# Instance normalisation over 64 tiles: six loads and six stores in turn, and a two-pass variance by pairs of tiles

## The chip, the cores and the metric

The kernel runs on one core of one Trainium2 chip. The metric is the device time in microseconds (us) of that core; lower is better. All runs compared here are with a granted clock of 1.0. A core has engines that run side by side: TensorE (PE in the profile), VectorE (DVE), ScalarE (ACT), GpSimd (POOL) and SyncE (SP). Here SP issues all DMAs, on one queue. Sixteen DMA engines do the moving. VectorE takes its instructions in the order in which the build put them; SP issues its DMAs in program order.

## The reference

```python
x = np.random.randn(8, 64, 32, 64, 64).astype(np.float32)      # 268 MB
mean = np.mean(x, axis=(2, 3, 4), keepdims=True)
var = np.var(x, axis=(2, 3, 4), keepdims=True)
out = (x - mean) / np.sqrt(var + 1e-5)
```

There are 512 instances (batch times channel) of 131,072 elements. Both kernels put 8 instances in a tile of 128 partitions by 8192 float32, which is 4 MiB, so there are 64 tiles. Every tile is loaded once and stored once.

## The kernel before

One tile is a group. Its sum (VectorE) and its sum of squares (ScalarE) are taken side by side, straight from the tile. A matmul with a block matrix adds the 16 partitions of each instance. A few small steps give scale and bias, and the normalising is shared by three engines. There are four tile buffers, and SP issues loads and stores alternately, with a store two tiles behind its load. The code is cut; `...` marks what is left out.

```python
c1 = F // 8; c2 = F // 4
norm_splits = [(nc.vector, 0, c1), (nc.scalar, c1, c2), (nc.gpsimd, c2, F)]
...
def issue_compute(g, x_tiles):
    for k in range(KPG):                                   # KPG is 1
        nc.vector.reduce_sum(out=psums[:, k, 0:1], in_=x_tiles[:, k, :], axis=...X)
        nc.scalar.activation(out=sq_scratch, in_=x_tiles[:, k, :], func=...Square,
                             accum_out=psums[:, k, 1:2])
    nc.tensor.matmul(out=tot, lhsT=ones_t, rhs=psums, start=True, stop=True)
    # ... mean, E[x^2] + eps - mean^2, square root, reciprocal, bias
    for eng, lo, hi in norm_splits: ...                    # x * scale + bias, in place
...
for g in range(n_groups):
    x_tiles = issue_load(g)
    issue_compute(g, x_tiles)
    pending[g] = x_tiles
    if g >= LAG:                                           # LAG is 2
        issue_store(g - LAG, pending.pop(g - LAG))
```

## Time and profile before

| | before |
|---|---|
| time, median | 1251.46 us (1250.81 to 1252.0, 3 runs) |
| span of the profiled run | 1249.7 us |
| DMA queue q1, share of 16 engines | 99.7% |
| moved | 536.88 MB, 430 GB/s |
| busiest compute engine | VectorE, 53% |

These are lines of the page of before: busy time, the queue line (packets, MB, share of the 16 engines' span), the chain of waits by engine, and three groups of instructions. A group's columns are: line, engine, operation, names, shapes and count; then busy us and the mean ns of one; then idle us before it and what ended that.

```profile
PE 35.7 (3%) x128; PEld 32.1 (3%) x128; DVE 659.2 (53%) x449; ACT 550.6 (44%) x258; POOL 380.3 (30%) x70
...
q1 hardware_dynamic: 18432, 536.88, 99.7%
...
DMA 74%; issue 16%; POOL 7%; DVE 1%; POOLq 1%; PE 0%; ACT 0%
...
L92 DVE TENSOR_REDUCE psums<-x_tiles 128x1 f32<-128x8192 f32 x64 | 555.9, 8686 | 492.9 <-DMA x_tiles<-in_x_dram 492.9
L100 ACT ACTIVATE sq_scratch<-x_tiles 128x8192 bf16<-128x8192 f32 x64 | 449.9, 7029 | 461.3 <-DMA x_tiles<-in_x_dram 461.3
L169 POOL TENSOR_SCALAR x_tiles<-x_tiles,scale,bias 128x6144 f32<-128x6144 f32 x64 | 379.4, 5929 | 855.4 <-DVE bias L149 634.4
```

The DMA engines are the bound: the queue is busy for 99.7% of the span, while VectorE and ScalarE sit waiting for loads.

The next lines are the chain of waits of before in order of time (start us, length us, what). They cover one period of four loads and four stores.

```profile
1023.82 31.48 DMA out_dram<-x_tiles
1055.30 0.02 issue
1055.32 26.52 DMA x_tiles<-in_x_dram
1081.84 13.26 issue
1095.10 0.04 POOLq L169
1095.15 0.12 issue
1095.27 5.95 POOL x_tiles L169
1101.21 0.02 issue
1101.23 31.49 DMA out_dram<-x_tiles
```

From 1023.82 to 1101.23 is 77.41 us for eight transfers of 4 MiB, so one transfer takes 9.68 us, and twelve would take 116.1 us. That pace is what a change would have to beat, or keep.

### The profile page before, as it was taken

The page shows a single profiled execution, that of the slowest core. Times are in us where ns is not written, and L with a number is a line of the kernel's source. Part 1 is how long each engine was busy: PE and PEld are TensorE (multiplying, and loading weights), DVE is VectorE, ACT ScalarE, POOL GpSimd, SP SyncE. Part 2 cuts the span into 40 slices and gives each one's busy share as a digit, 9 for nine tenths or more (in the row PEclk, how much of TensorE's full clock was granted, in tenths as well). Part 3 has the DMA queues.
Part 4 walks back from the last instruction along what each step waited for, and adds up shares of the span by engine and source line. Part 5 has one row for each costly group of instructions (what it writes and reads, how often), then busy time and mean ns, then how long its engine had stood idle before and what let it go on. Part 6 is the DMA issues. An engine that isn't in the chain of part 4 may idle for free.

```text
span 1249.7 us, 1827 instructions
## 1 busy us (share of the span) xinstructions
PE 35.7 (3%) x128; PEld 32.1 (3%) x128; DVE 659.2 (53%) x449; ACT 550.6 (44%) x258; POOL 380.3 (30%) x70
## 2 busy tenths in 40 slices
PE   0000000000000000000000000000000000000000
PEld 0000000000000000000000000000000000000000
DVE  5736455464554645546546455464554645646543
ACT  5535445354453544535435344354453544534432
POOL 2332332313323233232331322313323233132231
DMA  9999999999999999999999999999999999999998
GB/s 403 417 434 434 427 433 430 432 435 430 429 432 434 432 435 429 434 433 434 434 431 433 431 434 434 435 430 432 434 433 436 429 433 434 433 434 435 429 433 357
DMA packets 18444, 536.99 MB, mean 430 GB/s; under 512 B 2048, under 2 KB 2048, under 8 KB 2048
## 3 DMA queue, kind: packets, MB, share of 16 engines
q1 hardware_dynamic: 18432, 536.88, 99.7%
q14 instruction: 11, 0.09, 0.0%
q8 instruction: 1, 0.02, 0.0%
HBM read 268.44 MB, written 268.44 MB: 430 GB/s over the span
## 4 chain that ended last, share of the span: by engine, by line
DMA 74%; issue 16%; POOL 7%; DVE 1%; POOLq 1%; PE 0%; ACT 0%
DMA out_dram<-x_tiles 39%; DMA x_tiles<-in_x_dram 35%; POOL x_tiles L169 7%; DVE psums L92 1%; POOLq L221 0%; DVE x_tiles L169 0%; POOLq L169 0%; PE tot L108 0%; ACT std L141 0%; DVE scale L147 0%; DVE msq L128 0%; DVE me L117 0%; DVE bias L149 0%; DVE var_eps L131 0%
## 5 line engine op out<-in xcount | busy, mean ns | idle before, releaser
L92 DVE TENSOR_REDUCE psums<-x_tiles 128x1 f32<-128x8192 f32 x64 | 555.9, 8686 | 492.9 <-DMA x_tiles<-in_x_dram 492.9
L100 ACT ACTIVATE sq_scratch<-x_tiles 128x8192 bf16<-128x8192 f32 x64 | 449.9, 7029 | 461.3 <-DMA x_tiles<-in_x_dram 461.3
L169 POOL TENSOR_SCALAR x_tiles<-x_tiles,scale,bias 128x6144 f32<-128x6144 f32 x64 | 379.4, 5929 | 855.4 <-DVE bias L149 634.4
L161 ACT ACTIVATE x_tiles<-x_tiles,bias,scale 128x1024 f32<-128x1024 f32 x64 | 79.4, 1241 | 40.5 <-DVE bias L149 40.5
L141 ACT ACTIVATE std<-var_eps 128x1 f32<-128x1 f32 x64 | 13.0, 203 | 178.7 <-DVE var_eps L131 178.7
L108 PE MATMUL tot<-psums,ones_t 128*128 128x2 f32 x128 | 35.7, 348 | 1193.5 <-DVE psums L92 1193.5
L108 PEld LDWEIGHTS tot<-psums,ones_t 128*128 128x128 f32 x128 | 32.1, 311 | 1197.1 <-issue 1197.1
L169 DVE TENSOR_SCALAR x_tiles<-x_tiles,scale,bias 128x1024 f32<-128x1024 f32 x64 | 52.1, 813 | 2.5
L117 DVE TENSOR_SCALAR me<-tot 128x2 f32<-128x2 f32 x64 | 10.2, 160 | 47.5 <-PE tot L108 47.5
L147 DVE RECIPROCAL scale<-std 128x1 f32<-128x1 f32 x64 | 10.5, 164 | 21.8 <-ACT std L141 21.8
L100 ACT ACTIVATION_READ_ACCUMULATOR sq_scratch<-x_tiles 128x1 f32 x64 | 11.9, 187 | 0.0
L128 DVE TENSOR_TENSOR msq<-me 128x1 f32<-128x1 f32 x64 | 10.2, 159 | 2.2
L131 DVE SCALAR_TENSOR_TENSOR var_eps<-me,msq 128x1 f32<-128x1 f32 x64 | 10.2, 159 | 2.2
L149 DVE SCALAR_TENSOR_TENSOR bias<-me,scale 128x1 f32<-128x1 f32 x64 | 10.2, 159 | 2.2
L100 ACT ACT_TABLE_LOAD x1 | 1.3, 1283 | 0.8 <-PEq L207 0.8
L141 ACT ACT_TABLE_LOAD x1 | 1.3, 1283 | 0.0
L51 DVE MEMSET ones_t<- 128x128 f32 x1 | 0.2, 165 | 0.9 <-PEq L207 0.9
L53 POOL TENSOR_SCALAR_AFFINE_SELECT ones_t<-ones_t 128x128 f32<-128x128 f32 x1 | 0.3, 343 | 0.6 <-DVE ones_t L51 0.6
L62 POOL TENSOR_SCALAR_AFFINE_SELECT ones_t<-ones_t 128x128 f32<-128x128 f32 x1 | 0.3, 338 | 0.1
L207 POOL MEMSET const-float32-0.0<- 128x1 f32 x1 | 0.1, 98 | 0.3 <-issue 0.3
L207 POOL MEMSET const-bfloat16-1.0<- 128x1 bf16 x1 | 0.1, 101 | 0.0
L207 POOL MEMSET const-uint8-127<- 128x1 uint8 x1 | 0.1, 101 | 0.0
(1 smaller groups left out, 0.1 us busy)
## 6 DMA issues: line engine op xcount, KB each, us to landing
x_tiles<-in_x_dram SPq DMA_DIRECT2D x64, 4096.0 KB, 29.0
out_dram<-x_tiles SPq DMA_DIRECT2D x64, 4096.0 KB, 31.5
```

What stands on the lines that cost most here:

```text
L92: nc.vector.reduce_sum(out=psums[:, k, 0:1], in_=x_tiles[:, k, :], axis=mybir.AxisListType.X,)
L100: nc.scalar.activation(out=sq_scratch, in_=x_tiles[:, k, :], func=mybir.ActivationFunctionType.Square, accum_out=psums[:, k, 1:2],)
L108: nc.tensor.matmul(out=tot, lhsT=ones_t, rhs=psums, start=True, stop=True,)
L117: nc.vector.tensor_scalar(out=me2, in0=tot, scalar1=inv_F, scalar2=None, op0=mybir.AluOpType.mult,)
L128: nc.vector.tensor_mul(out=msq, in0=mean, in1=mean)
L131: nc.vector.scalar_tensor_tensor(out=var_eps, in0=e2, scalar=eps_f, in1=msq, op0=mybir.AluOpType.add, op1=mybir.AluOpType.subtract,)
L141: nc.scalar.activation(out=std, in_=var_eps, func=mybir.ActivationFunctionType.Sqrt,)
L147: nc.vector.reciprocal(out=scale, in_=std)
L149: nc.vector.scalar_tensor_tensor(out=bias, in0=mean, scalar=-1.0, in1=scale, op0=mybir.AluOpType.mult, op1=mybir.AluOpType.mult,)
L161: nc.scalar.activation(out=x_tiles[:, k, lo:hi], in_=x_tiles[:, k, lo:hi], func=mybir.ActivationFunctionType.Identity, scale=scale[:, k : ...
L169: eng.tensor_scalar(out=x_tiles[:, k, lo:hi], in0=x_tiles[:, k, lo:hi], scalar1=scale[:, k : k + 1], scalar2=bias[:, k : k + 1], op0=mybir ...
L207: nc = _bacc.Bacc("TRN2", target_bir_lowering=False, num_devices=1)
```

## The change

The intent is to keep the DMA in one direction for longer (six tiles in, six tiles out, six buffers), to use the safer two-pass variance, and to split the work by engine: VectorE sums, ScalarE squares, GpSimd normalises. Statistics are taken for two tiles at a time. The diff is cut to its core.

```diff
-    data_pool = ctx.enter_context(tc.tile_pool(name="data", bufs=4))
+    SLOTS = 6
+    BATCH = 2
+    data_pool = ctx.enter_context(tc.tile_pool(name="data", bufs=SLOTS))
 # ...
+    def compute(batch):
+        for k, t in enumerate(batch):
+            nc.vector.reduce_sum(out=sums[:, k : k + 1], in_=t, axis=...X)
+        nc.tensor.matmul(out=mean_ps, lhsT=avg, rhs=sums, start=True, stop=True)
+        nc.vector.tensor_scalar(out=neg_mean, in0=mean_ps, scalar1=-1.0, ..., op0=Alu.mult)
+        for k, t in enumerate(batch):
+            nc.scalar.activation(out=unused, in_=t, func=Act.Square,
+                                 bias=neg_mean[:, k : k + 1],
+                                 accum_out=squares[:, k : k + 1])
+        nc.tensor.matmul(out=var_ps, lhsT=avg, rhs=squares, start=True, stop=True)
+        nc.scalar.activation(out=std, in_=var_ps, func=Act.Sqrt, bias=eps_t)
+        nc.vector.reciprocal(out=scale, in_=std)
+        for k, t in enumerate(batch):
+            nc.gpsimd.tensor_scalar(out=t, in0=t, scalar1=neg_mean[:, k : k + 1],
+                                    scalar2=scale[:, k : k + 1], op0=Alu.add, op1=Alu.mult)
 # ...
+    loaded, stored = 0, 0
+    while stored < n_tiles:
+        load_and_compute(range(loaded, min(stored + SLOTS, n_tiles)))
+        loaded = min(stored + SLOTS, n_tiles)
+        turn = n_tiles % SLOTS or SLOTS if stored == 0 else SLOTS
+        for g in range(stored, stored + turn):
+            store(g, tiles.pop(g))
+        stored += turn
```

On SP this gives 6 loads, 4 stores, 4 loads, 6 stores, and then nine full turns of 6 loads and 6 stores. A pair is two tiles whose statistics are taken together, "sum3" is the sum of the third tile of a turn, and "recip12" is the reciprocal of the first pair.

More of the change, by code (lines that the diff above doesn't have):

```diff
@@ L4 @@
 import concourse.tile as tile
-from concourse import bass_utils, mybir
+from concourse import mybir
 from concourse._compat import with_exitstack
@@ L18 @@
     fp32 = mybir.dt.float32
+    Alu = mybir.AluOpType
+    Act = mybir.ActivationFunctionType
     P = 128
@@ L29 @@
     F = n_elem // SPLIT
-    G = 8
-    KPG = G // IPT
-    n_groups = n_inst // G
-    LAG = 2
-    x_packed = x.rearrange("b c d h w -> (b c) (d h w)").rearrange(
+    n_tiles = n_inst // IPT
+    SLOTS = 6
+    BATCH = 2
+    x_t = x.rearrange("b c d h w -> (b c) (d h w)").rearrange(
         "(k i) (s f) -> k (i s) f", i=IPT, s=SPLIT
     )
-    out_packed = out.rearrange("b c d h w -> (b c) (d h w)").rearrange(
+    out_t = out.rearrange("b c d h w -> (b c) (d h w)").rearrange(
         "(k i) (s f) -> k (i s) f", i=IPT, s=SPLIT
@@ L44 @@
     singles = ctx.enter_context(tc.tile_pool(name="singles", bufs=1))
-    data_pool = ctx.enter_context(tc.tile_pool(name="data", bufs=4))
-    scratch_pool = ctx.enter_context(tc.tile_pool(name="scratch", bufs=2))
+    data_pool = ctx.enter_context(tc.tile_pool(name="data", bufs=SLOTS))
     stat_pool = ctx.enter_context(tc.tile_pool(name="stats", bufs=4))
-    psum_pool = ctx.enter_context(tc.tile_pool(name="psum", bufs=4, space=bass.MemoryType.PSUM))
-    ones_t = singles.tile([P, P], fp32)
-    nc.vector.memset(ones_t, 1.0 / SPLIT)
-    blk_pattern = [[-SPLIT, P // SPLIT], [0, SPLIT]]
+    psum_pool = ctx.enter_context(
+        tc.tile_pool(name="psum", bufs=2, space=bass.MemoryType.PSUM)
+    )
+    avg = singles.tile([P, P], fp32, name="avg")
+    nc.vector.memset(avg, 1.0 / n_elem)
     nc.gpsimd.affine_select(
-        out=ones_t,
-        in_=ones_t,
-        pattern=blk_pattern,
-        compare_op=mybir.AluOpType.is_ge,
+        out=avg,
+        in_=avg,
+        pattern=[[-SPLIT, IPT], [0, SPLIT]],
+        compare_op=Alu.is_ge,
         fill=0.0,
@@ L62 @@
     nc.gpsimd.affine_select(
-        out=ones_t,
-        in_=ones_t,
-        pattern=[[SPLIT, P // SPLIT], [0, SPLIT]],
-        compare_op=mybir.AluOpType.is_ge,
+        out=avg,
+        in_=avg,
+        pattern=[[SPLIT, IPT], [0, SPLIT]],
+        compare_op=Alu.is_ge,
         fill=0.0,
@@ L70 @@
     )
-    inv_F = 1.0 / F
-    c1 = F // 8
-    c2 = F // 4
-    norm_splits = [
-        (nc.vector, 0, c1),
-        (nc.scalar, c1, c2),
-        (nc.gpsimd, c2, F),
-    ]
-    def issue_load(g):
-        x_tiles = data_pool.tile([P, KPG, F], fp32, name="x_tiles")
-        src = x_packed[g * KPG : (g + 1) * KPG].rearrange("k p f -> p k f")
-        nc.sync.dma_start(out=x_tiles, in_=src)
-        return x_tiles
-    def issue_compute(g, x_tiles):
-        psums = stat_pool.tile([P, KPG, 2], fp32, name="psums")
-        for k in range(KPG):
+    eps_t = singles.tile([P, 1], fp32, name="eps_t")
@@ L92, in issue_compute, with load, store @@
+    nc.vector.memset(eps_t, eps_f)
+    unused = singles.tile([P, F], mybir.dt.uint8, name="unused")
+    def load(g):
+        t = data_pool.tile([P, F], fp32, name="xt")
+        nc.sync.dma_start(out=t, in_=x_t[g])
+        return t
+    def store(g, t):
+        nc.sync.dma_start(out=out_t[g], in_=t)
+    def compute(batch):
+        n = len(batch)
+        sums = stat_pool.tile([P, n], fp32, name="sums")
+        for k, t in enumerate(batch):
             nc.vector.reduce_sum(
-                out=psums[:, k, 0:1],
@@ L94, in issue_compute @@
-                in_=x_tiles[:, k, :],
-                axis=mybir.AxisListType.X,
-            )
-            sq_scratch = scratch_pool.tile(
-                [P, F], mybir.dt.bfloat16, name="sq_scratch"
-            )
-            nc.scalar.activation(
-                out=sq_scratch,
-                in_=x_tiles[:, k, :],
-                func=mybir.ActivationFunctionType.Square,
-                accum_out=psums[:, k, 1:2],
-            )
-        tot = psum_pool.tile([P, KPG, 2], fp32, name="tot")
@@ L108, in issue_compute @@
-        nc.tensor.matmul(
-            out=tot,
-            lhsT=ones_t,
-            rhs=psums,
-            start=True,
-            stop=True,
-        )
-        me2 = stat_pool.tile([P, KPG, 2], fp32, name="me2")
-        nc.vector.tensor_scalar(
-            out=me2,
-            in0=tot,
-            scalar1=inv_F,
-            scalar2=None,
-            op0=mybir.AluOpType.mult,
-        )
-        mean = me2[:, :, 0]
-        e2 = me2[:, :, 1]
-        msq = stat_pool.tile([P, KPG], fp32, name="msq")
@@ L128, in issue_compute @@
-        nc.vector.tensor_mul(out=msq, in0=mean, in1=mean)
-        var_eps = stat_pool.tile([P, KPG], fp32, name="var_eps")
-        nc.vector.scalar_tensor_tensor(
-            out=var_eps,
-            in0=e2,
-            scalar=eps_f,
-            in1=msq,
-            op0=mybir.AluOpType.add,
-            op1=mybir.AluOpType.subtract,
-        )
-        std = stat_pool.tile([P, KPG], fp32, name="std")
-        nc.scalar.activation(
-            out=std,
-            in_=var_eps,
-            func=mybir.ActivationFunctionType.Sqrt,
-        )
@@ L146, in issue_compute @@
-        scale = stat_pool.tile([P, KPG], fp32, name="scale")
-        nc.vector.reciprocal(out=scale, in_=std)
-        bias = stat_pool.tile([P, KPG], fp32, name="bias")
-        nc.vector.scalar_tensor_tensor(
-            out=bias,
-            in0=mean,
-            scalar=-1.0,
-            in1=scale,
-            op0=mybir.AluOpType.mult,
-            op1=mybir.AluOpType.mult,
-        )
-        for k in range(KPG):
-            for eng, lo, hi in norm_splits:
-                if eng is nc.scalar:
-                    nc.scalar.activation(
-                        out=x_tiles[:, k, lo:hi],
-                        in_=x_tiles[:, k, lo:hi],
-                        func=mybir.ActivationFunctionType.Identity,
-                        scale=scale[:, k : k + 1],
-                        bias=bias[:, k : k + 1],
-                    )
-                else:
-                    eng.tensor_scalar(
-                        out=x_tiles[:, k, lo:hi],
-                        in0=x_tiles[:, k, lo:hi],
-                        scalar1=scale[:, k : k + 1],
-                        scalar2=bias[:, k : k + 1],
-                        op0=mybir.AluOpType.mult,
-                        op1=mybir.AluOpType.add,
-                    )
@@ L178, in issue_store @@
-    def issue_store(g, x_tiles):
-        dst = out_packed[g * KPG : (g + 1) * KPG].rearrange("k p f -> p k f")
-        nc.sync.dma_start(out=dst, in_=x_tiles)
-    pending = {}
-    for g in range(n_groups):
-        x_tiles = issue_load(g)
-        issue_compute(g, x_tiles)
-        pending[g] = x_tiles
-        if g >= LAG:
-            issue_store(g - LAG, pending.pop(g - LAG))
-    for g in range(n_groups - LAG, n_groups):
-        issue_store(g, pending.pop(g))
+                out=sums[:, k : k + 1], in_=t, axis=mybir.AxisListType.X
+            )
@@ new lines, in compute @@
+        mean_ps = psum_pool.tile([P, n], fp32, name="mean_ps")
+        nc.tensor.matmul(out=mean_ps, lhsT=avg, rhs=sums, start=True, stop=True)
+        neg_mean = stat_pool.tile([P, n], fp32, name="neg_mean")
+        nc.vector.tensor_scalar(
+            out=neg_mean, in0=mean_ps, scalar1=-1.0, scalar2=None, op0=Alu.mult
+        )
+        squares = stat_pool.tile([P, n], fp32, name="squares")
+        for k, t in enumerate(batch):
+            nc.scalar.activation(
+                out=unused,
+                in_=t,
+                func=Act.Square,
+                bias=neg_mean[:, k : k + 1],
+                accum_out=squares[:, k : k + 1],
+            )
@@ new lines, in compute @@
+        var_ps = psum_pool.tile([P, n], fp32, name="var_ps")
+        nc.tensor.matmul(out=var_ps, lhsT=avg, rhs=squares, start=True, stop=True)
+        std = stat_pool.tile([P, n], fp32, name="std")
+        nc.scalar.activation(out=std, in_=var_ps, func=Act.Sqrt, bias=eps_t)
+        scale = stat_pool.tile([P, n], fp32, name="scale")
+        nc.vector.reciprocal(out=scale, in_=std)
+        for k, t in enumerate(batch):
+            nc.gpsimd.tensor_scalar(
+                out=t,
+                in0=t,
+                scalar1=neg_mean[:, k : k + 1],
+                scalar2=scale[:, k : k + 1],
+                op0=Alu.add,
+                op1=Alu.mult,
+            )
@@ new lines, with load_and_compute @@
+    tiles = {}
+    def load_and_compute(group):
+        for g in group:
+            tiles[g] = load(g)
+        for g in range(group.start, group.stop, BATCH):
+            compute([tiles[h] for h in range(g, min(g + BATCH, group.stop))])
+    loaded, stored = 0, 0
[6 more added lines that the diff above has]
+        stored += turn
```

## The prediction

> **What bounds it now: the DMA engines.** Queue line: q1 99.7% of 16 engines' span, at 430 GB/s; the busiest compute engine, VectorE, is at 53%. In the chain of waits, 4 loads and 4 stores take 77.4 us (1023.82 to 1101.23): 9.68 us per 4 MiB tile, 433 GB/s. In the packets each 32 KB row takes 1213 ns, for loads and stores alike. The Trainium skill, "DMA: Bandwidth & Descriptors", section "Where 436 GB/s comes from", puts the ceiling at 435.2 GB/s; 433 agrees. The pure loading at the start (tiles 0 to 2) runs at the same 9.68 us. So grouping the directions six by six should gain nothing: there is no turnaround cost to save.
>
> **What the change does.** Bytes, rows and queue are unchanged. Does the queue still always have work? SP issues in order; a group's first store waits for its normalising, and the next group's loads stand behind all six stores. Loads can't fill a wait for a late store.
>
> Costs from the groups of instructions: sum 8.69 us; square 7.03 + 0.19 to read the accumulator; normalising wholly on GpSimd, 5.93 x 8192/6144 = 7.9 us (estimate); matmul pair 0.56, small VectorE step 0.16, root 0.20; store issue to first packet 1.5 us (29.91 to 31.39).
>
> Two-pass variance makes a chain per pair: second sum 8.7, matmul and mean 0.9, two squares 14.4, matmul, root, reciprocal 1.1, normalising 7.9 + 7.9. Squares now follow the sums. The build orders VectorE: sum1 sum2 mean12 | sum3 recip12 sum4 mean34 | sum5 recip34 sum6 mean56 | recip56. So sum4 waits for recip12, hence for both squares of the first pair, and sum6 for recip34. The pairs are serialised, about 25.2 us from recip to recip (8.7 + 0.9 + 14.4 + 1.1), though two loads take only 19.4.
>
> With a group's first load at 0 (estimate): tile 2 lands at 19.8; recip12 at 45; tiles 1, 2 normalised at 53, 61; recip34 at 70; tiles 3, 4 at 78, 86; recip56 at 95; tiles 5, 6 at 103.5, 111.4. The queue wants the stores at 58.1, 67.8, 77.4, 87.1, 96.8, 106.5. Stores 1 and 2 make it. Store 3 is ready for its packets at 79.8: 2.4 us idle. Store 5 at 105 against 99.2: 5.8 us more.
>
> Idle per full turn is about 8.2 us, times 9 turns, plus 2.4 us in each of the two shorter first turns: 75 to 80 us, all on the critical path. [...]
>
> **Predicted: 1328 us (+6%), 80% range 1300 to 1350.** Faster by over 2%: 0.01; within 2%: 0.07; slower by over 2%: 0.92.
>
> **What the profile would show.** Right: q1's share falls to about 94%; the chain of waits shows VectorE, ScalarE and GpSimd pieces before the third and fifth store of each turn; SP waits on GpSimd there; sum4 and sum6 start after a reciprocal that ScalarE released, not at their load; packets still take 1213 ns. Wrong: q1 at 99% (the pairs overlap more than I think), or packets off 1213 ns (direction matters).
>
> **What would make it wrong.** A square 0.2 us longer adds about 12 us in all, one 0.2 us shorter takes as much away. GpSimd may not scale with length. Writing squares as 8-bit into one shared tile may change ScalarE's time or add a wait. If long one-way stretches run faster, the idle is partly paid back.

## The result, and the profile after

| | before | after |
|---|---|---|
| time, median | 1251.73 us (4 runs) | 1322.77 us (1322.68 to 1322.98, 4 runs) |
| ratio | 1 | 1.0568 (95%: 1.0553 to 1.0583) |
| span of the profiled run | 1249.7 us | 1320.9 us |
| q1's share of 16 engines | 99.7% | 95.6% |
| idle of the queue (span less share x span) | 3.7 us | 58.1 us |

A ratio is the mean time of one kernel's fast runs over that of the other's in the same rounds, so it is not quite the ratio of the medians quoted.

These are the same lines of the page, of the changed kernel.

```profile
PE 37.5 (3%) x128; PEld 32.0 (2%) x128; DVE 563.8 (43%) x130; ACT 472.7 (36%) x162; POOL 459.2 (35%) x70
...
q1 hardware_dynamic: 18432, 536.88, 95.6%
...
issue 32%; DMA 25%; DVE 20%; ACT 11%; POOL 6%; PE 2%; SPq 1%; POOLq 1%; ACTq 0%; DVEq 0%
...
L113 POOL TENSOR_SCALAR xt<-xt,neg_mean,scale 128x8192 f32<-128x8192 f32 x64 | 458.3, 7172 | 846.1 <-DVE scale L111 639.9
L99 ACT ACTIVATE unused<-xt,neg_mean 128x8192 uint8<-128x8192 f32 x64 | 455.8, 7122 | 784.7 <-DVE neg_mean L94 774.0
L88 DVE TENSOR_REDUCE sums<-xt 128x1 f32<-128x8192 f32 x64 | 555.5, 8679 | 390.5 <-DMA xt<-in_x_dram 390.0
```

All three compute engines are far from full, and VectorE and ScalarE are busy for less time than before, yet the kernel is slower. What changed is the chain: the DMA's part fell from 74% to 25%, and VectorE and ScalarE now hold 20% and 11% of it. ScalarE used to wait for loads and now waits for the mean (784.7 us idle, 774.0 of it for `neg_mean`).

Two shares of busy time separate the loss. Before, the queue was busy for 99.7% of 1249.7 us, or 1246.0 us; after, for 95.6% of 1320.9 us, or 1262.8 us. So of the 71.2 us more span, about 54.4 us are an idle queue and about 16.8 us are packets that took longer. (The page gives the shares to 0.1%, so each product is good to some 0.6 us; the packets of the two traces add up to 1246.5 and 1262.8 us, which makes it 54.9 and 16.3.)

The next lines are windows of one full turn of the changed kernel. The columns are the window, its length, then busy us (and instructions) of PE, PEld, DVE, ACT and POOL, PE's clock, the DMA's share and GB/s.

```profile
463.30:521.40 58.10, 2.35 (x8) 2.01 (x8) 41.92 (x10) 29.38 (x10) 14.86 (x3) 1.00 1.01 433
521.40:549.00 27.60, 1.17 (x4) 1.00 (x4) 8.21 (x3) 14.69 (x5) 16.75 (x3) 1.00 0.93 399
549.00:554.00 5.00, 0.00 (x0) 0.00 (x0) 0.00 (x0) 0.00 (x0) 5.00 (x2) 1.00 0.00 0
554.00:587.60 33.60, 0.00 (x0) 0.00 (x0) 2.66 (x1) 0.00 (x0) 6.36 (x1) 1.00 1.01 421
```

Between 549 and 554 us nothing moves at all: every engine is idle but GpSimd, which ends the fifth tile at 553.2 us and begins the sixth, and SP waits to issue the fifth store. A share over 1.00 comes from a packet's time being counted in the window where it starts.

The timeline of VectorE in the same turn shows why the fifth tile is late (start us, length us, engine, line, operation; in brackets the idle before it and what ended that).

```profile
495.36 0.17 DVE L111 RECIPROCAL scale<-std 128x2 f32<-128x2 f32 x1 [6.65 <-ACT std L109]
495.44 8.67 DVE L88 TENSOR_REDUCE sums<-xt 128x1 f32<-128x8192 f32 x1
504.86 0.16 DVE L94 TENSOR_SCALAR neg_mean<-mean_ps 128x2 f32<-128x2 f32 x1 [0.75 <-PE mean_ps L92]
504.96 8.69 DVE L88 TENSOR_REDUCE sums<-xt 128x1 f32<-128x8192 f32 x1
520.54 0.17 DVE L111 RECIPROCAL scale<-std 128x2 f32<-128x2 f32 x1 [6.89 <-ACT std L109]
520.62 8.67 DVE L88 TENSOR_REDUCE sums<-xt 128x1 f32<-128x8192 f32 x1
530.04 0.16 DVE L94 TENSOR_SCALAR neg_mean<-mean_ps 128x2 f32<-128x2 f32 x1 [0.75 <-PE mean_ps L92]
545.71 0.17 DVE L111 RECIPROCAL scale<-std 128x2 f32<-128x2 f32 x1 [15.52 <-ACT std L109]
```

The sum at 495.44 (the fourth tile) and the sum at 520.62 (the sixth) start right behind a reciprocal that had waited 6.65 and 6.89 us for ScalarE's root. Their data had landed: neither line names a load as what ended a wait. From reciprocal to reciprocal it is 25.2 us (495.36, 520.54, 545.71), as predicted, where two loads take 19.4. The Trainium skill, "PSUM — Partial Sum Buffer", section "Engine vs sequencer instructions", says that the queues of ScalarE, VectorE and GpSimd "are strict FIFO"; these lines of VectorE agree (the sum at 520.62 begins behind the reciprocal at 520.54). The small instruction holds the large one up, though the large one does not need its result.

The predicted schedule of a turn against the measured one, in us from the first packet of the turn's first load (449.86 in this trace, read from its packets):

| | predicted | measured |
|---|---|---|
| recip12, recip34, recip56 | 45, 70, 95 | 45.5, 70.7, 95.9 |
| tiles 3 and 4 normalised | 78, 86 | 78.2, 85.3 |
| tiles 5 and 6 normalised | 103.5, 111.4 | 103.3, 110.5 |
| queue empty before the third and the fifth store (measured: mean of the 16 engines, from the packets) | 2.4, 5.8 | 0.6, 5.6 |
| length of a full turn | 116.2 + 8.2 | 124.3 |

### The profile page after: what moved, and what is told of

Same layout as the page of the kernel before. It is cut to its first block, busy times and chain, and to the rows that moved or that the text cites. A ratio compares the mean times of both kernels' runs of the same rounds, so it can differ in the third digit from the quotient of the medians.

```text
span 1320.9 us, 1106 instructions
## 1 busy us (share of the span) xinstructions
PE 37.5 (3%) x128; PEld 32.0 (2%) x128; DVE 563.8 (43%) x130; ACT 472.7 (36%) x162; POOL 459.2 (35%) x70
## 3 DMA queue, kind: packets, MB, share of 16 engines
q1 hardware_dynamic: 18432, 536.88, 95.6%
## 4 chain that ended last, share of the span: by engine, by line
issue 32%; DMA 25%; DVE 20%; ACT 11%; POOL 6%; PE 2%; SPq 1%; POOLq 1%; ACTq 0%; DVEq 0%
DMA xt<-in_x_dram 25%; DVE sums L88 19%; ACT unused L99 11%; POOL xt L113 6%; PE mean_ps L92 1%; POOLq L170 1%; SPq L78 1%; PE var_ps L107 1%; ACT std L109 0%; DVE neg_mean L94 0%; SPq L82 0%; DVE scale L111 0%; ACTq L99 0%; DVEq L94 0%; POOLq L113 0%
## 5 line engine op out<-in xcount | busy, mean ns | idle before, releaser
L113 POOL TENSOR_SCALAR xt<-xt,neg_mean,scale 128x8192 f32<-128x8192 f32 x64 | 458.3, 7172 | 846.1 <-DVE scale L111 639.9
L99 ACT ACTIVATE unused<-xt,neg_mean 128x8192 uint8<-128x8192 f32 x64 | 455.8, 7122 | 784.7 <-DVE neg_mean L94 774.0
L88 DVE TENSOR_REDUCE sums<-xt 128x1 f32<-128x8192 f32 x64 | 555.5, 8679 | 390.5 <-DMA xt<-in_x_dram 390.0
L111 DVE RECIPROCAL scale<-std 128x2 f32<-128x2 f32 x32 | 5.3, 166 | 312.9 <-ACT std L109 312.9
L92 PE MATMUL mean_ps<-sums,avg 128*128 128x2 f32 x64 | 18.8, 363 | 778.4 <-DVE sums L88 778.4
L92 PEld LDWEIGHTS mean_ps<-sums,avg 128*128 128x128 f32 x64 | 16.0, 311 | 781.1 <-DVE sums L88 749.3
L107 PE MATMUL var_ps<-squares,avg 128*128 128x2 f32 x64 | 18.8, 363 | 475.4 <-ACT unused L99 475.4
L107 PEld LDWEIGHTS var_ps<-squares,avg 128*128 128x128 f32 x64 | 16.0, 311 | 478.2 <-ACT unused L99 478.2
L109 ACT ACTIVATE std<-var_ps,eps_t 128x2 f32<-128x2 f32 x32 | 8.4, 262 | 21.0 <-PE var_ps L107 21.0
L99 ACT ACTIVATION_READ_ACCUMULATOR unused<-xt,neg_mean 128x1 f32 x64 | 12.0, 187 | 0.0
```

The source lines that it names most:

```text
L88: nc.vector.reduce_sum(out=sums[:, k : k + 1], in_=t, axis=mybir.AxisListType.X)
L92: nc.tensor.matmul(out=mean_ps, lhsT=avg, rhs=sums, start=True, stop=True)
L99: nc.scalar.activation(out=unused, in_=t, func=Act.Square, bias=neg_mean[:, k : k + 1], accum_out=squares[:, k : k + 1],)
L107: nc.tensor.matmul(out=var_ps, lhsT=avg, rhs=squares, start=True, stop=True)
L109: nc.scalar.activation(out=std, in_=var_ps, func=Act.Sqrt, bias=eps_t)
L111: nc.vector.reciprocal(out=scale, in_=std)
```

## The experiments

Theory A is the prediction's: the reciprocal in VectorE's queue makes the pairs serial, so the third and fifth store of a turn come late; the next loads stand behind all six stores, so nothing fills the gap. Rival B is that long one-way stretches, or their turns, are slower for the memory or the DMA engines. Rival C is that GpSimd, normalising whole tiles alone, is what makes the stores late. In every run below the ratio is against before, in the same rounds.

### e1 and e2: the same instructions in another order on VectorE

e1 puts the reciprocal of a pair behind the next pair's mean, by an edge that orders two instructions of one engine and costs no semaphore. e2 does the opposite and puts both sums of a pair behind the reciprocal of the pair before.

```diff
-            compute([tiles[h] for h in range(g, min(g + BATCH, group.stop))])
+            made = compute([...])                 # now returns its mean and its reciprocal
+            if g > group.start:
+                tc.add_manual_dep(last[1].ins, made[0].ins.name, <NoSync edge>, ...)  # e1
+            last = made
 # e2, instead:  for s in this pair's two sums: tc.add_manual_dep(s.ins, last[1].ins.name, ...)
```

> Same instructions as the changed kernel; only VectorE's order differs: the reciprocal of a pair stands behind the next pair's two sums and mean, by an ordering edge without a semaphore. Theory A (the 0.17 us reciprocal holds the next sum back, so the pairs are serial and stores 3 and 5 of a turn come late): the idle before both stores goes, a turn takes 116 to 117 us instead of 124.3, 1246 to 1256 us in all. Rival B (six loads then six stores is itself slower for the memory or the DMA engines): stays within 10 us of 1323. Rival C (GpSimd's normalising of the whole tile, 7.2 us each, is what makes the stores late): stays above 1300.

> The opposite dose: same instructions, but both sums of a pair stand behind the reciprocal of the pair before. Theory A: the distance from reciprocal to reciprocal grows by one sum, 25.2 to 33.9 us, so store 3 comes 8.7 us later and store 5 17.4 us later: 124.3 + 17.4 = 141.7 us per full turn, 9 turns, and 8.7 us in each of the two shorter first turns: 1323 + 157 + 17 = 1497 us, range 1470 to 1520. Rivals B and C: no change, 1313 to 1333.

e1 measured 1256.9 us (ratio 1.0041, 95%: 1.0024 to 1.0057), and e2 1495.28 us (1.1945). The queue line of e1, and of e2:

```profile
q1 hardware_dynamic: 18432, 536.88, 99.9%
```

```profile
q1 hardware_dynamic: 18432, 536.88, 84.5%
```

The timeline of VectorE in e1, in a turn:

```profile
597.79 0.16 DVE L94 TENSOR_SCALAR neg_mean<-mean_ps 128x2 f32<-128x2 f32 x1 [0.75 <-PE mean_ps L92]
597.87 0.16 DVE L111 RECIPROCAL scale<-std 128x2 f32<-128x2 f32 x1
598.13 8.69 DVE L88 TENSOR_REDUCE sums<-xt 128x1 f32<-128x8192 f32 x1
607.78 8.69 DVE L88 TENSOR_REDUCE sums<-xt 128x1 f32<-128x8192 f32 x1 [0.96 <-DMA xt<-in_x_dram]
```

In e1 the reciprocal no longer waits for ScalarE, and the sum at 607.78 waits for its load alone. The same work takes 66 us less. In e2 each pair is one sum longer; its timeline has reciprocals at 1006.51 and 1040.30, 33.8 us apart (33.9 expected), and the total is 1.7 us from the forecast of 1497. Both directions of one edit move the time by about the amounts of theory A; B and C had no reason for either. e1's 1256.9 lies 0.9 us over its expected range; that rest is taken up with e9 to e11.

### e3: loads and stores in sixes with almost no computing

```diff
-        (sums, means, squares, variance, root, reciprocal)
             nc.gpsimd.tensor_scalar(
-                out=t, in0=t, scalar1=neg_mean[:, k : k + 1], scalar2=scale[:, k : k + 1], ...
+                out=t[:, 0:1], in0=t[:, 0:1], scalar1=eps_t, scalar2=eps_t, ...
```

> Wrong result on purpose: all statistics are taken out and GpSimd touches one column of each tile, so loads and stores in sixes run with almost no computing behind them. Theory A: the queue is never empty within the kernel, 1243 to 1252 us, 9.68 us per tile in both directions. Rival B (long one-way stretches or their turns cost time): 1290 us or more.

Measured: 1251.22 us, ratio 0.9994 (0.998 to 1.0009). Its output is wrong, which doesn't matter for the time. (It passes the comparison all the same, for the reason given at e7.) These lines of its page are the busy times and the queue:

```profile
DVE 0.2 (0%) x2; POOL 22.7 (2%) x70
...
q1 hardware_dynamic: 18432, 536.88, 99.8%
```

Rival B falls as a cause by itself: sixes cost nothing where the queue does not run empty (what a turn of direction costs where it does is taken up with e10). They gain nothing either, so what the grouping by direction was to save was not there. With almost no computing left the time is the same as before's, so less computing would not make this kernel clearly faster.

### e4: one-pass variance in the changed kernel

```diff
+            nc.scalar.activation(out=unused, in_=t, func=Act.Square, accum_out=sums[:, 1, k : k + 1])
+        # one matmul for both; var + eps = E[x^2] + eps - mean^2
-        (squares with bias=neg_mean after the mean, second matmul)
```

> One-pass variance (sums and squares side by side, mean of squares less squared mean) in the otherwise changed kernel: same slots, pairs, sixes on SP and GpSimd normalising. Theory A: squares no longer follow the sums, so the chain from a pair's landing to its reciprocal is about 11 us instead of 25; all stores are in time: 1246 to 1256 us. Rival B or C: stays above 1300.

Measured: 1251.73 us, ratio 0.9998 (0.9983 to 1.0013), correct, with the queue busy for 99.8% of the span. Squares that do not wait for the mean take the chain away, with pairs, sixes and GpSimd as changed.

### e5: the changed computing under an alternating queue

```diff
-    (six loads, six stores in turn)
+    for g in range(0, n_tiles, BATCH):
+        for h in range(g, g + BATCH): tiles[h] = load(h)
+        compute([tiles[h] for h in range(g, g + BATCH)])
+        for h in range(g - LAG, g - LAG + BATCH):          # LAG is 4
+            if h >= 0: store(h, tiles.pop(h))
```

> The changed kernel's computing untouched (two passes, pairs, reciprocal in VectorE's queue as the build puts it), but SP's order is two loads, two stores, stores four tiles behind, with the same six slots. Theory A says that late stores cost only because six loads stand behind six stores: a pair's serial chain is at most about 34 us (17.4 sums, 0.9, 14.4, 1.1) and two loads and two stores take 38.7, so the queue never runs empty: 1247 to 1257 us. Rival (the two-pass computing alone is too slow for the queue whatever the order): above 1300.

Measured: 1251.8 us, ratio 1.0 (0.9986 to 1.0015). The two-pass computing is fast enough as it stands: the serial chain costs time only where six loads stand behind six stores. So two things are needed together, the chain by pairs and the queue in sixes; taking either away is enough. The chain is still there in e5, as these lines of its page show:

```profile
q1 hardware_dynamic: 18432, 536.88, 99.7%
...
L111 DVE RECIPROCAL scale<-std 128x2 f32<-128x2 f32 x32 | 5.3, 166 | 479.7 <-ACT std L109 479.7
```

The reciprocals wait for ScalarE for 479.7 us in all, more than in the changed kernel (312.9), because the build puts each one ahead of both sums of the next pair here, as e2 does. It costs nothing: at 517.00 us a reciprocal is done with its wait, and the next pair's first sum starts at 521.07, at the landing of its load.

### e6 and e7: a shorter square, a shorter normalising

```diff
-                out=unused, in_=t, func=Act.Square, ...
+                out=unused[:, 0 : 7 * F // 8], in_=t[:, 0 : 7 * F // 8], func=Act.Square, ...   # e6
-                out=t, in0=t, scalar1=neg_mean...
+                out=t[:, 0 : 3 * F // 4], in0=t[:, 0 : 3 * F // 4], scalar1=neg_mean...          # e7
```

> Wrong result on purpose: squares over 7/8 of each row, 6.2 us instead of 7.1; all else as changed. Theory A: the serial part of a pair is 1.8 us shorter, so store 3 comes 1.8 us earlier (its idle goes) and store 5 3.6 us earlier; a full turn takes about 119 us instead of 124.3, in all 1272 us, range 1262 to 1285. If ScalarE's time were not on the chain: 1323.

> Wrong result on purpose: GpSimd normalises 3/4 of each row (6144 elements, as before the change); all else as changed. Theory A: normalising enters a late store once, not once per pair, so each late store comes 1.8 us earlier and the idle of a turn falls by 1.8 us only: 1322.8 - 9 x 1.8 - 2 = 1305 us, range 1298 to 1312. Rival C (normalising is what makes the pairs late): the gain doubles or more, below 1290. Beside that: if 6144 elements take 5.4 us here (7.16 x 3/4) and not the 5.93 of the kernel before, the rest there came from something running beside it.

Their outputs are wrong, which doesn't matter for the times. (e7 still passes the comparison, because the input is drawn with mean 0 and variance 1, so the quarter left alone is already nearly normal.) e6 measured 1272.79 us, 50.0 us less than the changed kernel; e7 1304.11 us, 18.7 us less. The groups of ScalarE in e6 and of GpSimd in e7:

```profile
L99 ACT ACTIVATE unused<-xt,neg_mean 128x7168 uint8<-128x7168 f32 x64 | 401.1, 6268 | 789.7 <-DVE neg_mean L94 779.0 <-issue 9.7
```

```profile
L113 POOL TENSOR_SCALAR xt<-xt,neg_mean,scale 128x6144 f32<-128x6144 f32 x64 | 349.1, 5465 | 935.1 <-DVE scale L111 664.1 <-issue 271.0
```

A square is 0.85 us shorter in e6 (7122 to 6268 ns), normalising 1.71 us in e7 (7172 to 5465 ns). The square, with half the saving per instruction, gives over twice the gain. That is what a serial chain does: before the fifth store six squares stand on it, but only one normalising. The first sums of two turns of e6 start at 565.79 and 685.00 us, so a turn takes 119.21 us, 5.13 less than the changed kernel's 124.34 (460.60 to 584.94), and six times 0.854 is 5.12. (The expectation named 3.6 us for the fifth store, which counted four squares. The 119 us that it gave for the turn was right by luck: it took off 1.8 us for the third store and 3.6 for the fifth, 5.4 in all, which is near the 5.1 that six squares make.) Rival C falls: GpSimd is on the chain, once per late store.

### e8: statistics tile by tile

```diff
-    BATCH = 2
+    BATCH = 1
```

> Statistics tile by tile instead of by pairs (VectorE: sum1 mean1 sum2 recip1 mean2 sum3 recip2 and so on); all else as changed. Theory A: the serial part per tile is about 8.7 + 0.9 + 7.2 + 1.1 = 18 us less what now overlaps (the next sum runs beside the squares), below the 9.7 us per tile only if they overlap; from the order I expect about 10 us per tile and all stores in time: 1246 to 1260 us. If the pairs' serial chain were not the cause: about 1323.

Measured: 1251.85 us, ratio 0.9998 (0.9981 to 1.0014), correct. The timeline of VectorE:

```profile
461.29 8.69 DVE L88 TENSOR_REDUCE sums<-xt 128x1 f32<-128x8192 f32 x1
469.89 0.15 DVE L111 RECIPROCAL scale<-std 128x1 f32<-128x1 f32 x1
470.72 0.16 DVE L94 TENSOR_SCALAR neg_mean<-mean_ps 128x1 f32<-128x1 f32 x1 [0.68 <-PE mean_ps L92]
471.00 8.69 DVE L88 TENSOR_REDUCE sums<-xt 128x1 f32<-128x8192 f32 x1
```

Here a tile's square runs beside the next tile's sum, so when the reciprocal comes up in VectorE's queue its root is ready and it waits for nothing. A sum starts every 9.7 us (461.29 to 471.00), the pace of a load. One changed digit takes the loss back.

### e9 to e11: packets that take longer, only half settled

The 16.8 us of longer packets are not explained by the chain, and e1 had some too: its queue is hardly ever idle (99.9%), but its packets take 99.9% of 1254.0, or 1252.7 us, against 1246.0 us before. Most packets take 1213 ns in all kernels. In the changed kernel the long ones stand together at the turns of direction: near 572.4 us, from storing to loading, all 16 engines have one packet of 1.7 to 2.3 us, and near 630.2 us, from loading to storing, nine of them have one of 1.4 to 2.0 us. Added up per engine, the two turns cost about 0.9 and 0.5 us. At the restart of the empty queue at 554.06 us no packet takes over 1.26 us. In e1, after its first 140 us, only the turns from storing to loading cost something (0.4 to 0.9 us per engine).

e9 is e1 with e6's shorter squares, e1_again is e1 on the same chip.

> Wrong result on purpose: e1 (late reciprocal) with squares over 7/8 of each row, 6.3 us instead of 7.1, so every store is issued 2 to 4 us before the queue comes to it instead of 1.0 us. e1 had no idle queue but was 0.4% slower than before, with packets that took 6.8 us longer in all. If that rest came from stores issued only just in time: 1249 to 1253 us, the same as before within 0.2%, and the queue's packet time falls to 1246 to 1248 us. If it comes from VectorE's order or from the turns of direction as such: 1255 to 1258 us.

> The kernel of e1 again, as the pair of e9 on the same chip: 1256 to 1258 us, about 0.4% over before, if its rest is real and not of one chip.

e9 measured 1256.56 us (ratio 1.0032, 95%: 1.0019 to 1.0044), e1 again 1257.08 us (1.0038, 1.0025 to 1.0052). So the 0.4% of e1 is real. But e9 did not do what it was made for: in its trace the packets of the first and third store of a turn still start 0.8 to 1.5 us after their issue, as in e1, since the late reciprocal waits for the second pair's sums and loads and not for squares. It decides nothing about stores issued just in time. (In the changed kernel a store that finds the queue empty starts 0.8 us after its issue, so e1's and e9's queues are close to empty at those stores; every store of e4 and e8 starts 16 us or more after its issue.)

e10 is e3 with the fourth store of a turn held back, so that the queue runs empty; e11 is e1 with a few extra loads on half of the engines.

```diff
+            if slow and k == 1:                            # e10: second pair of a turn of six
+                for _ in range(7): nc.gpsimd.tensor_scalar(out=t, in0=t, ...)
+            if g in (25, 27, 49, 51):                      # e11: after these stores
+                nc.sync.dma_start(out=junk[part : part + 8, :], in_=x_t[0][0:8, 0:1536])
```

> Wrong result on purpose: e3 (almost no computing, sixes), but seven whole-tile passes on GpSimd hold back the fourth store of each turn of six loads, so that the queue runs empty for about 4 us once per turn, ten times, as it does in the changed kernel. After an empty queue all 16 engines start in step. Theory D (the packets of 1.3 to 2.3 us come at turns of direction when the engines are in step): packet time rises from e3's 1245.7 to 1256-1263 us, with the long packets at the turns and not at the restarts, about 1307 us in all. Theory E (packet time goes with the amount of computing, or with store latency): packet time stays at 1245 to 1248 us, about 1292 us in all.

> e1 (late reciprocal) with four extra loads of 8 rows of 6 KB into an unused tile, two of them in each of two turns (about 1/3 and 2/3 of the way); a load of 8 rows runs on half of the engines alone and puts them about 0.2 us behind, 0.45 us per turn. Theory D: the long packets at the turns right after these shrink to under half of what the turns before show (0.6 to 0.8 us per engine), and total packet time falls by 1 to 4 us; the total time may hardly change, since the extra loads cost 0.9 us. Theory E: the turns stay as they are.

e10 measured 1305.91 us (ratio 1.0433). Its queue line:

```profile
q1 hardware_dynamic: 18432, 536.88, 96.7%
```

Its packets take 96.7% of 1304.2, or 1261.2 us, against 1245.7 us in e3 (99.8% of 1248.2); the rest of the loss, 43.0 us, is the idle queue. So with hardly any computing, an empty queue once per turn is enough to bring the longer packets. They stand at the turns again: about 0.8 to 0.9 us per engine from storing to loading, mostly 0.5 to 0.7 from loading to storing. e10 holds a control of its own: its second turn, of four loads, was not held back, and the next two turns of direction, near 203 and 261 us, have no packet over 1.25 us. e10 also rules out stores issued just in time as the only cause: at the turn near 503 us the store had been issued 48 us ahead (458.5 for 506.2), and the turn cost 0.6 us all the same.

Theory D explained this by engines in step, and e11 does not bear that out. It measured 1258.31 us (ratio 1.0053), and the turn right after its first extra loads, near 548 us, cost 1.1 us per engine instead of less; the next three from storing to loading cost 0.7, 0.7 and 0.6, about as the turns before them did. The turn after the second extra loads, near 1018 us, cost 1.0. But e11 is no clean test: the edit puts the extra loads behind the fourth and the last store of a turn, not at a third and two thirds as expected, so the second of them stands in the turn of direction itself (its packets, at 550.5 to 551.0 us, lie among the long ones). Being in step is not enough in any case: in e1 the 16 engines start their packets within 0.33 us of each other some 5 us ahead of the turn near 256 us, which costs nothing, and within 0.56 us ahead of the one near 548 us, which costs 0.5. So it is shown that an empty queue is followed by costly turns of direction; how, and why e1 has them with a queue that is hardly ever empty while e4 and e8 do without (packet time 1246.6 and 1246.7 us), stays open.

## Why the prediction was right, and which terms were off

- **The bound and the gain from sixes.** "Grouping the directions six by six should gain nothing": e3 measured 1251.22 against 1251.37 us. The Trainium skill, "DMA: Bandwidth & Descriptors", section "Where 436 GB/s comes from", gives 435.2 GB/s as the ceiling of the 16 memory ports that the DMA engines share; before's period of 77.41 us for 33.55 MB is 433 GB/s, so there was hardly anything above to reach for.
- **The serial pairs.** The build's order on VectorE was read before the run, and the step of 25.2 us from reciprocal to reciprocal was measured as 25.2. e1 and e2 move that order alone, and the time follows both ways.
- **On the critical path in full.** Loads behind six stores cannot fill the gap; e5 alternates them and the loss is gone.
- **Sensitivity.** "A square 0.2 us longer adds about 12 us": e6's 0.85 us took 50.0 us, which is 11.7 per 0.2.
- **Sizes.** 1328 was forecast and 1322.77 measured, but two terms were off and partly cancelled, so that the total came so close is in part luck. The 1328 is before's 1251 us and about 77 us of idle. Idle was forecast as 75 to 80 us and is 54.4 more than before. Most of the miss is the third store: 2.4 us of idle per turn were forecast, and 0.6 measured; for the fifth, 5.8 and 5.6. Normalising takes 7.17 us, not 7.9, and a store's first packet comes 0.82 us after its issue (553.24 to 554.06), not 1.5; the 1.5 had been read where the queue was still busy with a load. So the third store was ready about 0.8 us earlier than forecast, and the queue came to it about 1 us later, because packets ahead of it took longer. The other term is those packets: "packets still take 1213 ns" holds for most of them, but at the turns of direction they took up to 2.3 us, which cost 16.8 us in all. By the prediction's own sign, "packets off 1213 ns (direction matters)", this part of it was wrong. "There is no turnaround cost to save" holds for before and e3, but the changed kernel, with its empty queue, got one. q1's share, forecast as 94%, is 95.6% for the same reason: part of the cost shows as packet time and not as idle.
- **Why 7.9 was wrong.** It scaled 5.93 us by the length. e3's normalising of one element takes 340 ns, and e7's of 6144 takes 5465; so there is a fixed 0.34 us and about 1.2 elements per ns, which gives 7.17 for 8192. Before's 5.93 has 0.46 us more than e7's at the same length. There a VectorE `tensor_scalar` of 0.81 us had started 0.2 us ahead (552.72 and 552.93), and ScalarE's share of the tile ran beside it too. The Trainium skill, "SBUF — State Buffer", section "Who interferes with whom", says that such an operation can take the port pair that VectorE shares with GpSimd, which then blocks. The 0.46 us would fit that, but no run took that operation away alone, so it is not shown.

## What to carry to other kernels

Read the order in which a build puts instructions on an in-order engine: a 0.17 us instruction that waits for another engine holds every large instruction behind it, and busy shares of 43% do not show it. Where all loads stand behind all stores of a turn on one queue, the slowest store's latency counts in full, so either alternate them or see to it that each tile is ready before the queue comes to its store. Grouping transfers by direction is worth trying only if the trace shows that alternating costs something; here loads and stores took 9.68 us each in either order.

## What the Trainium skill lacked or had wrong

- "DMA: Bandwidth & Descriptors", section "Where 436 GB/s comes from", says that for HBM to SBUF the HBM side (about 358 GB/s) binds, though a table of the same page has 425 for a core alone. With one core running, e3 and before moved 430 GB/s over the whole span, and before 433 in the steady part. "HBM Reference", section "Specifications (TRN2)", has it right for a core alone, at about 425.
- No page that I found says what a change of direction costs on one queue. Alternating and sixes measured 1251.37 and 1251.22 us. Where the queue had run empty in the same turn (the changed kernel, e10), a change of direction cost about 0.4 to 0.9 us on each engine, with packets of up to 2.3 us instead of 1.213; no page has this, and no run here shows the mechanism.
- "GPSIMD Engine Reference", section "Elementwise — side-by-side cycle accounting", has cycles per element and a measured addition of two tensors, but no measured `tensor_scalar`, and no time for the fixed part of one. Here it is 0.34 us and 1 us more for each 1200 elements per partition (340 ns for 1, 5465 for 6144, 7172 for 8192).
- That VectorE's queue is strictly first in, first out is said in passing on pages about other things, "PSUM — Partial Sum Buffer" among them. No page that I found says what follows: a 0.17 us instruction that waits there delays a large independent one, 66 us in all in this kernel (1322.77 against e1's 1256.9). It deserves a place where VectorE is described.
